# Moving ScalarE's low-half gate copies from behind their one-hots into the next two weight chunks

## The chip, the cores and the metric

The kernel runs on one core of a Trainium2 chip. The core has five engines that run beside each other, each through its own instructions in the order in which they were written down: TensorE (PE, matmuls into PSUM), VectorE (DVE), ScalarE (ACT), GpSimd (POOL, here the indirect row gathers) and SyncE (SP, here nearly all other transfers). An engine that comes to an instruction whose input is not there waits, and all behind it on that engine waits too. The metric is the time of one execution in microseconds (us); lower is better.

## The reference, cut to what matters

One layer of a streaming encoder block over 512 tokens of width 1024: a mixer with two head groups, then a channel sub-layer that picks single-neuron experts, then a norm. The change touches the expert part alone:

```
q = (xb @ w_q).reshape(p, PEER_HEADS, 2, PEER_DK_HALF)
sc = jnp.einsum('phcd,hcnd->phcn', q, sub_keys).astype(jnp.float32)
top_s, top_i = lax.top_k(sc, PEER_TOPK)
cand_s = (top_s[:, :, 0, :, None] + top_s[:, :, 1, None, :]).reshape(p, PEER_HEADS, kk)
cand_i = (top_i[:, :, 0, :, None] * N_KEYS + top_i[:, :, 1, None, :]).reshape(p, PEER_HEADS, kk)
best_s, best_pos = lax.top_k(cand_s, PEER_TOPK)
idx = jnp.take_along_axis(cand_i, best_pos, axis=-1)
g = jax.nn.softmax(best_s, axis=-1)
u_sel = expert_u[idx]
act = jax.nn.gelu(jnp.einsum('phkd,pd->phk', u_sel, xb), approximate=False)
coef = (g * act.astype(jnp.float32)).astype(xb.dtype)
return jnp.einsum('phk,phkd->pd', coef, expert_v[idx])
```

Each token has 8 heads with 16 experts each, 128 of the 16384 = 128 x 128 experts. An expert is named by a pair of numbers, one from each half of the keys.

## The kernel before

**Dense and sparse tokens.** 192 of the 512 tokens are handled sparsely: their experts' rows are fetched by indirect DMA (L753) and VectorE takes dot products with them (L774). The other 320 tokens are handled densely: all 16384 activations are computed as matmuls with the whole of `expert_u`, and the picked ones are kept by multiplying with a gate matrix that is zero elsewhere.

**The u chunks.** `expert_u` comes in 128 chunks of 512 KB. The matmuls work with a split: ScalarE copies a chunk to a rounded high half (`whi`, `w_high`, L78), VectorE subtracts to get the low half (`wlo`, `w_low`, L83), and TensorE does three products per block, 24 matmuls in all (L92 to L94), into one of two accumulators (`ps_act`, `bufs=2`). ScalarE empties the accumulator with a gelu (`u_evict`, L841); this is written down one chunk later, so chunk k's matmuls need the eviction of chunk k - 2, which stands in ScalarE's list in chunk k - 1.

**The gates.** For 8 tokens at a time a gate step (`gates_step`) prepares and multiplies. The preparation (`gates_prep`) has VectorE make one-hots of both key numbers (L626) and multiply one of them with the high part of the gate (L631); ScalarE makes the same product with the low part of the gate, in eight copies with a scale (L633 and L634, the "low copies"). They go to the second half of the tile `igh`. The gate matmuls (`gates_mm`, L645) use high and low product, and they are written down one gate step later than the preparation. The gate evictions to a staging tile (`gates_out`, L654) and the store of a full tile (`gates_store`, L665) follow one step after that. There are 40 such steps of 8 tokens, and at the end 16 of 4 tokens in another form without low copies.

**The order of the work** is written out by hand (`manual_schedule`). The loop over the first `CE` = 124 chunks writes down, for chunk k: the load of chunk k + 5 on SyncE and the low half of chunk k + 2 on VectorE (`weights`), chunk k's matmuls and the eviction of chunk k - 1 (`u_chunk`), then VectorE work from four generators (searches, rest of the searches, gates, dots) until the planner's counter of VectorE time has caught up with TensorE's, and last the high half of chunk k + 3 (`w_high`). The planner chooses by counters (`pe`, `dve`, `ac`) and due times, all fixed when the program is built. Most gate steps fall into every second chunk, some into neighbouring ones. In ScalarE's list one chunk with a gate step thus reads: eviction of chunk k - 1, eight low copies, two gate evictions of the step before, high half of chunk k + 3.

After these chunks come the rest of u and the 128 chunks of `expert_v` (L1020), not touched by the change.

Of the kernel before, what the change touches and what calls it, by code (L numbers as in the profile page):

```python
# [2 lines left out]

# [10 lines left out]
AF = mybir.ActivationFunctionType  # L14
# [20 lines left out]
def block_kernel(ctx, tc, xT, small, w_ada1, w_ada, b_ada, w_in, w_r, w_i, w_out, w_q, keys, uT, u, v, final_g, out):  # L35
    nc = tc.nc
# [53 lines left out]
    def mm3(ps, hi, lo, xh, xl, ks, first, last):  # L90
        for k in ks:
            nc.tensor.matmul(ps, hi[:, k, :], xh(k), start=first and k == ks[0], stop=False)  # L92
            nc.tensor.matmul(ps, hi[:, k, :], xl(k), start=False, stop=False)  # L93
            nc.tensor.matmul(ps, lo[:, k, :], xh(k), start=False, stop=last and k == ks[-1])  # L94
# [226 lines left out]
    for cb in range(4):  # L321
# [16 lines left out]
        ig = mt("ig")  # L338
# [274 lines left out]
    def gates_prep(sl, t0, wide):  # L613
        oh = topk.tile([128, 8, 128], F32, name="oh8", bufs=2)
        if not wide:
            nc.vector.tensor_tensor(oh[:, 0:4, :], iota[:, None, :].to_broadcast([128, 4, 128]),
                                    sl[:, 1, t0:t0 + 4, None].to_broadcast([128, 4, 128]), op=OP.is_equal)
            for k in range(4):
                nc.vector.tensor_scalar(oh[:, 4 + k, :], iota, sl[:, 0, t0 + k:t0 + k + 1], sl[:, 2, t0 + k:t0 + k + 1],
                                        op0=OP.is_equal, op1=OP.mult)  # L620
            return oh, None
        sij, gh, gl = sl
        flat = oh.rearrange("p a b -> p (a b)").bitcast(F16)
        a0 = slice(t0 // 2, t0 // 2 + 4)
        shp = [128, 8, 128, 2]
        nc.vector.tensor_tensor(flat.rearrange("p (q n b) -> p q n b", q=8, b=2), io2[:, None, :, :].to_broadcast(shp),  # L626
                                sij[:, a0].rearrange("p a w b -> p (a w) b")[:, :, None, :].to_broadcast(shp),
                                op=OP.is_equal)
        of = flat.rearrange("p (a w n b) -> p a w n b", a=4, w=2, b=2)
        ig = topk.tile([128, 2, 4, 128, 2], F16, name="igh", bufs=2)  # L630
        nc.vector.tensor_tensor(ig[:, 0], of[:, :, 0], gh[:, a0][:, :, None, :].to_broadcast([128, 4, 128, 2]), op=OP.mult)  # L631
        for k in range(8):
            nc.scalar.activation(ig[:, 1, k // 2, :, k % 2], of[:, k // 2, 0, :, k % 2], AF.Copy,  # L633
                                 scale=gl[:, t0 + k:t0 + k + 1])  # L634
        return of, ig

    def gates_mm(oh, ig, k0):
        pg = psE.tile([128, 4, 128], F32, name="ps_gt", bufs=4)
        for k in range(4):
            a, b = divmod(k0 + k, 2)  # L640
            if ig is None:
                nc.tensor.matmul(pg[:, k, :], oh[:, k, :], oh[:, 4 + k, :], start=True, stop=True)
            else:
                for w in range(2):
                    nc.tensor.matmul(pg[:, k, :], oh[:, a, 1, :, b], ig[:, w, a, :, b], start=w == 0, stop=w == 1)  # L645
        return pg
# [3 lines left out]
    def gates_out(t, t0, pg, scale):  # L650
        gq, q4 = divmod(t0 // 4, 4)
        if q4 == 0:
            gst[t] = stgp[0].tile([128, 128, 16], F32, name="stg", bufs=2)
        nc.scalar.activation(gst[t][:, :, q4 * 4:q4 * 4 + 4], pg.rearrange("p t n -> p n t"), AF.Copy, scale=scale)  # L654
        if q4 == 3:
            stores.append((t, gq, gst[t]))
# [3 lines left out]
    def gates_store():  # L660
        while stores:
            t, gq, st = stores.pop()
            for e in (1, 0):
                eng = nc.scalar if (t, gq) == (1, 3) else nc.sync
                eng.dma_start(Gd[t][gq][:, 64 * e:64 * e + 64, :], st[:, 64 * e:64 * e + 64, :])  # L665

    def gates_step(item):
        if item is not None:
            t, sl, t0, wide = item
            gpre.append((t, t0, gates_prep(sl, t0, wide)))  # L670
        gates_store()
        for _ in range(len(gpost)):
            gates_out(*gpost.pop(0))
        if len(gpre) > (item is not None):
            t, t0, (oh, ig) = gpre.pop(0)
            for k0 in range(0, 4 if ig is None else 8, 4):
                gpost.append((t, t0 + k0, gates_mm(oh, ig, k0), 1.0 if ig is None else 1.0 / GS))
                pe[0] += 890 if ig is None else GPE

    def gates_tile(t, groups, sl, wide=True):  # L680
        step = 8 if wide else 4
        for t0 in range(groups[0] * 16, groups[-1] * 16 + 16, step):
            gates_step((t, sl, t0, wide))
            ac[0] += 510 * step if wide else 120 * step
            given["g"] += step // 4
            yield 1780 if wide else 1680
# [63 lines left out]
    def gath(table, idxs, k, key):  # L750
        if key not in rows:
            r = row_tile()
            nc.gpsimd.indirect_dma_start(out=r[:, :], out_offset=None, in_=table,  # L753
                                         in_offset=bass.IndirectOffsetOnAxis(ap=idxs[:, k:k + 1], axis=0))
            rows[key] = r
# [59 lines left out]
    def w_high(k):  # L815
        if k < len(jobs):
            whi[k] = high(wraw[k])
# [5 lines left out]
    def weights(k):  # L823
        w_load(k + 5)
        w_low(k + 2)
# [4 lines left out]
    def spill(q):  # L830
        nc.sync.dma_start(Ad[q], act[q].rearrange("p c t -> p (c t)"))
        act[q] = None
# [3 lines left out]
    def u_evict():  # L836
        if unread:
            c, ps = unread.pop()
            if c % 2 == 0:
                act[c // 2] = ring.tile([128, 2, NU], F32, name="act", bufs=RB // 2)  # L840
            nc.scalar.activation(act[c // 2][:, c % 2], ps, AF.Gelu)  # L841

    def u_chunk(k, pool):
        c = jobs[k][1]
        ps = pool.tile([128, NU], F32, name="ps_act", bufs=2)
        mm3(ps, whi.pop(k), wlo.pop(k), hd, ld, range(KB), True, True)
        u_evict()
        unread.append((c, ps))
        q = c // 2 - RB // 2 + 2
        if c % 2 == 0 and 0 <= q < v0 // 2:  # L850
            spill(q)
        pe[0] += 3530
        dve[0] += 1140
        ac[0] += 1400
# [99 lines left out]
    for k in range(CE):  # L954
        weights(k)
        u_chunk(k, psE)
        cur[0] = k
        if sready and not first:
            first.append(k + 4)
            asleep["d"] = k + 4  # L960
            for m in range(GB_E - 1):
                gath(u, usteps[m][0], usteps[m][3], m)
        ac[0] = max(ac[0], pe[0] - LEAD)
        dve[0] = max(dve[0], RHO * pe[0] - LEAD - (HEAD if k < 9 else 0))
        xd = 0
        while dve[0] < RHO * pe[0] or k == KD:
            g = turn(k)
            if k == KD:
                g = next((g for g in "sg" if g in gens), None)
                if "s" not in gens and len(bdone) < XB:  # L970
                    g = "d"
            if g is None or (g == "d" and "g" not in gens and xd >= XD):
                break
            n = next(gens[g], 0)
            if n == 0:
                assert g != "d"
                late_k[g] = k
                del gens[g]
                continue
            if n is None:  # L980
                asleep[g] = k + 1
                continue
            dve[0] += n
            xd += g == "d"
            if gopen or g == "d":
                given[g] += {"g": 0, "d": 1}.get(g, n)
        w_high(k + 3)
        if k == KD:
            ep.close()
            vp = ctx.enter_context(tc.tile_pool(name="vp", bufs=2, reuse_waits="tile"))  # L990
            gp = ctx.enter_context(tc.tile_pool(name="gp", bufs=1, reuse_waits="tile"))
            late[:] = [gp, taken[0] + 10]
            gt8 = vp.tile([128, 2, NG, 8, 16], F32, name="gt", bufs=1)
        m = k - CE + XE
        if 0 <= m < XE:
            for n in [0] if m < 2 else range(5) if m == XE - 1 else [8]:
                v_gates(n)
        if m >= XE - 2:
            (v_gated, v_rest)[m - XE + 2](0)
# [37 lines left out]
    for k in range(CE, len(jobs)):  # L1037
# [3 lines left out]
        kind, n = jobs[k]  # L1041
# [25 lines left out]
    g2r, _, fgr = frow  # L1067
# [107 lines left out]
```

## Time and profile before

| what | us |
|---|---|
| median of 3 runs (lowest, highest) | 1497.47 (1497.16, 1499.59) |
| the profiled execution: time, span | 1498.0, 1496.2 |
| TensorE matmul busy | 1352.5 (90%) |
| VectorE busy | 1225.6 (82%) |
| ScalarE busy | 686.6 (46%) |
| GpSimd busy | 507.3 (34%) |
| high halves L78, ScalarE | 308.4 |
| low halves L83, VectorE | 356.0 |
| dots L774, VectorE (192 of them) | 234.5 |
| one-hots L626, VectorE | 48.8 |

Busy times overlap, since the engines run beside each other. A row of a costly group reads: line, engine, operation, output and inputs with shapes, count, then busy time and the mean in ns of one, then the idle time of that engine just before these instructions and what ended most of it. A row of the list of waits reads: engine and line that waited, engine and line that it waited for, total us, times, longest. In a timeline row stand start and length in us, and in brackets the idle time before it. In a row of windows the columns are named in its first line; "PEclk" is the clock granted to TensorE as a share of full speed, "DMA share" the busy share of the core's 16 DMA engines.

### The profile page before, as it was taken

Reading aid. Unit: us, or ns where it says so; the run is one execution under the profiler, and the core shown is the slowest. Engines: PE = TensorE matmul, PEld = TensorE weight load, DVE = VectorE, ACT = ScalarE, POOL = GpSimd, SP = SyncE. Lnnn points to the kernel's source line nnn. Section 1 sums busy time; section 2 is a strip of 40 time slices with the busy share of each in tenths; the row PEclk is TensorE's granted clock in tenths of the full one; section 3 lists DMA queues with packets and bytes.
Section 4 is the critical chain, followed back from the end, with each engine's and each line's share of the span. In section 5 each row is a group of like instructions: output and inputs, shape, how many; then the busy total and the mean of one; then the engine's idle time right before and its main releaser. Section 6 shows DMA issues by size and latency. Waiting matters only on the chain.

```text
span 1496.2 us, 21797 instructions
## 1 busy us (share of the span) xinstructions
PE 1352.5 (90%) x7739; PEld 1158.2 (77%) x7739; DVE 1225.6 (82%) x2332; ACT 686.6 (46%) x1178; POOL 507.3 (34%) x334
## 2 busy tenths in 40 slices
PE   5999999989888877878788997999999999999996
PEld 2666786889888877878777996787788888888885
DVE  6765655999787767878777997698998899999998
ACT  4544434444456566566555442334334343333333
POOL 0000000001132023231445355465666575555540
PEclk9999999999999898999999998999999999999998
DMA  9666222235577778888999999999999999999994
GB/s 375 215 234 211 95 89 71 85 113 168 184 232 267 243 241 289 284 268 280 312 360 326 355 388 381 339 381 378 415 410 414 408 416 413 414 414 402 391 338 164
DMA packets 146929, 440.07 MB, mean 294 GB/s; under 512 B 14722, under 2 KB 42370, under 8 KB 144772
## 3 DMA queue, kind: packets, MB, share of 16 engines
q1 hardware_dynamic: 99812, 267.75, 49.8%
q0 software_dynamic: 46720, 169.89, 29.8%
q8 instruction: 60, 0.98, 0.3%
q10 hardware_dynamic: 288, 1.05, 0.2%
q14 instruction: 49, 0.40, 0.1%
HBM read 393.54 MB, written 45.09 MB: 293 GB/s over the span
## 4 chain that ended last, share of the span: by engine, by line
PE 41%; issue 26%; DVE 13%; DMA 12%; POOL 7%; ACT 1%; DVEq 0%; POOLq 0%; SPq 0%; ACTq 0%
PE acc L1020 26%; POOL rows L753 7%; DMA rows<-in_u_dram,idx_s 6%; DMA wraw<-in_v_dram 4%; PE ps_z L92 4%; PE ps_z L94 4%; PE ps_z L93 4%; DVE wlo L83 2%; DVE scr L774 2%; DMA rows<-in_u_dram,idx_b 1%; PE ps_row L136 1%; DVE rep L457 1%; DVE ti L455 1%; DVE ti L462 1%; DVE top L460 1%
## 5 line engine op out<-in xcount | busy, mean ns | idle before, releaser
L78 ACT ACTIVATE whi<-wraw 128x1024 fp32r<-128x1024 f32 x292 | 308.4, 1057 | 427.1 <-PE acc L1020 174.0
L83 DVE TENSOR_TENSOR wlo<-wraw,whi 128x1024 fp32r<-128x1024 f32 x292 | 356.0, 1221 | 174.2 <-ACT whi L78 173.0
L92 PE MATMUL ps_act<-h,whi 128*128 128x320 f32 x1024 | 334.7, 327 | 83.3 <-ACT act L841 82.1
L94 PE MATMUL ps_act<-h,wlo 128*128 128x320 f32 x1024 | 325.0, 317 | 2.9 <-DVE wlo L83 2.9
L93 PE MATMUL ps_act<-h,whi 128*128 128x320 f32 x1024 | 324.9, 317 | 0.0
L92 PEld LDWEIGHTS ps_act<-h,whi 128*128 128x128 f32 x1024 | 200.6, 196 | 93.0 <-ACT act L841 91.4
L753 POOL DMA_INDIRECT rows<-in_u_dram,idx_s x128 | 201.5, 1574 | 168.0 <-DVE scr L774 145.2
L753 POOL DMA_INDIRECT rows<-in_v_dram,idx_s x128 | 203.6, 1591 | 155.3 <-DVE ys L790 136.2
L1020 PE MATMUL acc<-whi,ch 128*128 128x512 f32 x750 | 232.6, 391 | 11.4 <-ACT act L841 10.7
L1020 PE MATMUL acc<-whi,cl 128*128 128x512 f32 x750 | 232.2, 391 | 3.0 <-DVE cl L917 2.8
L1020 PE MATMUL acc<-wlo,ch 128*128 128x512 f32 x750 | 232.1, 391 | 0.4 <-DVE wlo L83 0.4
L753 POOL DMA_INDIRECT rows<-in_u_dram,idx_b x64 | 97.0, 1515 | 344.6 <-DVE scr L774 260.6
L94 PEld LDWEIGHTS ps_act<-h,wlo 128*128 128x128 f32 x1024 | 200.0, 195 | 3.5 <-DVE wlo L83 3.4
L93 PEld LDWEIGHTS ps_act<-h,whi 128*128 128x128 f32 x1024 | 201.0, 196 | 0.2
L633 ACT ACTIVATE igh<-oh,gl 128x128 f16<-128x128 f16 x320 | 99.7, 428 | 162.2 <-DVE oh L626 162.2
L1020 PEld LDWEIGHTS acc<-whi,ch 128*128 128x128 f32 x750 | 140.9, 188 | 41.9 <-ACT act L841 11.5
L774 DVE SCALAR_TENSOR_TENSOR scr<-rows,h2n 128x1024 f16<-128x1024 f32 x128 | 156.4, 1222 | 18.0 <-DMA rows<-in_u_dram,idx_s 16.6
L1020 PEld LDWEIGHTS acc<-whi,cl 128*128 128x128 f32 x750 | 140.8, 188 | 34.6 <-DVE cl L917 5.5
L1020 PEld LDWEIGHTS acc<-wlo,ch 128*128 128x128 f32 x750 | 141.3, 188 | 30.3 <-DVE wlo L83 0.8
L790 DVE SCALAR_TENSOR_TENSOR ys<-rows,acts,ys 128x1024 f32<-128x1024 f32 x127 | 162.7, 1281 | 1.4
L408 POOL DMA_DIRECT2D x1d<-xn x8 | 4.5, 568 | 281.1 <-DVE wlo L83 234.4
L92 PE MATMUL ps_z<-h,whi 128*128 128x512 f32 x224 | 90.8, 409 | 2.7 <-ACT h L216 2.4
(261 smaller groups left out, 1684.6 us busy)
## 6 DMA issues: line engine op xcount, KB each, us to landing
wraw<-in_uT_dram SPq DMA_DIRECT2D x128, 512.0 KB, 6.0
wraw<-in_v_dram SPq DMA_DIRECT2D x128, 512.0 KB, 9.3
Gd<-stg SPq DMA_DIRECT2D x46, 512.0 KB, 7.4
wada<-in_w_ada_dram SPq DMA_DIRECT2D x16, 1024.0 KB, 5.3
Ad<-act SPq DMA_DIRECT2D x48, 320.0 KB, 6.6
act<-Ad SPq DMA_DIRECT2D x48, 320.0 KB, 11.4
h<-Gd SPq DMA_DIRECT2D x12, 1024.0 KB, 15.7
wraw<-in_w_in_dram SPq DMA_DIRECT2D x20, 512.0 KB, 6.3
```

Source lines behind the costliest of these rows:

```text
L78: nc.scalar.activation(hi, raw, AF.Copy)
L83: nc.vector.tensor_sub(lo, raw, hi.bitcast(F32))
L92: nc.tensor.matmul(ps, hi[:, k, :], xh(k), start=first and k == ks[0], stop=False)
L93: nc.tensor.matmul(ps, hi[:, k, :], xl(k), start=False, stop=False)
L94: nc.tensor.matmul(ps, lo[:, k, :], xh(k), start=False, stop=last and k == ks[-1])
L136: nc.tensor.matmul(pr[32 * b:32 * b + 1, :], cs[:, k:k + 1], wt[:, b * 512:(b + 1) * 512], start=(k == 0), stop=(k == KB - 1), skip_group_ ...
L455: nc.vector.max_index(out=where[:, 0:8], in_max=best[:, 0:8], in_values=s)
L633: nc.scalar.activation(ig[:, 1, k // 2, :, k % 2], of[:, k // 2, 0, :, k % 2], AF.Copy, scale=gl[:, t0 + k:t0 + k + 1])
L753: nc.gpsimd.indirect_dma_start(out=r[:, :], out_offset=None, in_=table, in_offset=bass.IndirectOffsetOnAxis(ap=idxs[:, k:k + 1], axis=0))
L774: nc.vector.scalar_tensor_tensor(scr, rows.pop(n), 1.0, hn, op0=OP.mult, op1=OP.mult, accum_out=dst[:, k:k + 1])
L790: nc.vector.scalar_tensor_tensor(ys, rows.pop(k), acts[:, k:k + 1], ys, op0=OP.mult, op1=OP.add)
L1020: nc.tensor.matmul(accs[b][e], st[:, bs], mv[:, e * 512:(e + 1) * 512], start=first, stop=last)
```

## The change

`gates_prep` no longer writes down the eight low copies; it puts the tiles that they need on a list. A new function `gates_low(n)` writes down up to n copies from that list, oldest first. It is called with 4 in each u chunk, right behind that chunk's `u_chunk`, and with 8 ahead of each gate step, so that a step's copies stand before the gate matmuls that read them and before the next preparation. The counters of the planner are not changed.

```diff
-from itertools import chain
+from itertools import chain, cycle
...
-        for k in range(8):
-            nc.scalar.activation(ig[:, 1, k // 2, :, k % 2], of[:, k // 2, 0, :, k % 2], AF.Copy,
-                                 scale=gl[:, t0 + k:t0 + k + 1])
+        lows.append((of, ig, gl, t0))
         return of, ig
+
+    lows = []
+
+    def gates_low(n):
+        for _ in range(n):
+            if lows:
+                of, ig, gl, t0 = lows[0]
+                k = next(low_k)
+                nc.scalar.activation(ig[:, 1, k // 2, :, k % 2], of[:, k // 2, 0, :, k % 2], AF.Copy,
+                                     scale=gl[:, t0 + k:t0 + k + 1])
+                if k == 7:
+                    lows.pop(0)
+
+    low_k = cycle(range(8))
...
         for t0 in range(groups[0] * 16, groups[-1] * 16 + 16, step):
+            gates_low(8)
             gates_step((t, sl, t0, wide))
...
         u_chunk(k, psE)
+        gates_low(4)
         cur[0] = k
```

## The prediction

> **What bounds the kernel now.** I read the page's costliest groups first, then the list of waits cut into the stretch where the changed line runs, then one period of that stretch in the timeline, engine by engine.
>
> ```profile
> L83 DVE TENSOR_TENSOR wlo<-wraw,whi 128x1024 fp32r<-128x1024 f32 x292 | 356.0, 1221 | 174.2 <-ACT whi L78 173.0
> L92 PE MATMUL ps_act<-h,whi 128*128 128x320 f32 x1024 | 334.7, 327 | 83.3 <-ACT act L841 82.1
> L633 ACT ACTIVATE igh<-oh,gl 128x128 f16<-128x128 f16 x320 | 99.7, 428 | 162.2 <-DVE oh L626 162.2
> L1020 PE MATMUL acc<-whi,ch 128*128 128x512 f32 x750 | 232.6, 391 | 11.4 <-ACT act L841 10.7
> ```
>
> Three waits form a ring. ScalarE stands 162.2 us in front of the low copies (L633) until VectorE has the one-hot; TensorE stands 82.1 us in front of a new u chunk until ScalarE has emptied an accumulator (L841); VectorE stands 173.0 us until ScalarE has made a high half (L78). The 320 low copies are 40 gate steps of eight. The answer for their line gives durations (min/median/max) and the first and last start:
>
> ```profile
> L633 ACT ACTIVATE igh<-oh,gl x320: 418/426/448, 387.3 to 806.6; 128x128 f16<-128x128 f16 x160
> ```
>
> Only between 387 and 807 us does the change act. The list of waits over three stretches of it:
>
> ```profile
> PE ps_act L92 <- ACT act L841: 39.2, 13, 7.0
> DVE wlo L83 <- ACT whi L78: 50.9, 19, 6.0
> PE ps_act L92 <- ACT act L841: 16.9, 9, 3.1
> DVE wlo L83 <- ACT whi L78: 16.1, 8, 3.1
> PE ps_act L92 <- ACT act L841: 23.1, 11, 3.6
> DVE wlo L83 <- ACT whi L78: 22.8, 11, 2.9
> ```
>
> The pairs of rows are 387 to 600, 600 to 700 and 700 to 820 us (total, times, longest). TensorE's 39.2, 16.9 and 23.1 add to 79.2, nearly all of the 82.1: here lies what can be won. Busy times of the same stretches, and of two later ones:
>
> ```profile
> core 0: us, PE busy (x) PEld busy (x) DVE busy (x) ACT busy (x) POOL busy (x), PEclk, DMA share, GB/s
> 387.00:600.00 213.00, 171.22 (x1228) 166.16 (x1229) 160.06 (x334) 131.62 (x289) 51.83 (x35) 0.90 0.74 245
> 600.00:700.00 100.00, 83.15 (x625) 79.74 (x624) 78.45 (x169) 61.50 (x137) 31.34 (x20) 0.97 0.84 284
> 700.00:820.00 120.00, 96.90 (x726) 92.98 (x725) 92.46 (x125) 68.92 (x160) 53.93 (x35) 0.99 0.92 326
> 820.00:900.00 80.00, 76.32 (x551) 76.08 (x550) 73.52 (x146) 34.37 (x53) 35.69 (x25) 0.98 0.99 372
> 1200.00:1300.00 100.00, 100.00 (x443) 82.81 (x442) 94.44 (x88) 40.79 (x52) 62.67 (x37) 1.00 1.03 414
> ```
>
> Neither TensorE nor VectorE is full between 387 and 820 us, each at about 75 to 83%: they wait for each other in turn, through ScalarE. One period, two u chunks with one gate step, ScalarE first, then VectorE, then TensorE:
>
> ```profile
> 724.18 1.05 ACT L78 ACTIVATE whi<-wraw 128x1024 fp32r<-128x1024 f32 x1
> 725.13 0.43 ACT L841 ACTIVATE act<-ps_act 128x320 f32<-128x320 f32 x1
> 730.00 2.49 ACT L633 ACTIVATE igh<-oh,gl 128x128 f16<-128x128 f16 x8 [4.45 <-DVE oh L626]
> 732.36 1.05 ACT L654 ACTIVATE stg<-ps_gt 128x512 f32<-128x512 f32 x2
> 733.31 1.05 ACT L78 ACTIVATE whi<-wraw 128x1024 fp32r<-128x1024 f32 x1
> 734.26 0.42 ACT L841 ACTIVATE act<-ps_act 128x320 f32<-128x320 f32 x1
> ```
>
> ```profile
> 724.00 1.23 DVE L83 TENSOR_TENSOR wlo<-wraw,whi 128x1024 fp32r<-128x1024 f32 x1 [2.62 <-ACT whi L78]
> 725.14 1.22 DVE L774 SCALAR_TENSOR_TENSOR scr<-rows,h2b 128x1024 f16<-128x1024 f32 x1
> 728.69 1.22 DVE L626 TENSOR_TENSOR oh<-io,selT 128x2048 f16<-128x2048 f16 x1
> 734.39 1.23 DVE L83 TENSOR_TENSOR wlo<-wraw,whi 128x1024 fp32r<-128x1024 f32 x1 [2.62 <-ACT whi L78]
> 736.80 1.22 DVE L774 SCALAR_TENSOR_TENSOR scr<-rows,h2b 128x1024 f16<-128x1024 f32 x1
> ```
>
> ```profile
> 724.34 0.42 PE L92 MATMUL ps_act<-h,whi 128*128 128x320 f32 x1 [2.11 <-ACT act L841]
> 727.96 1.09 PE L645 MATMUL ps_gt<-igh,oh 128*128 128x128 f16 x16
> 734.73 0.41 PE L92 MATMUL ps_act<-h,whi 128*128 128x320 f32 x1 [2.11 <-ACT act L841]
> ```
>
> The chain can be followed by its start times: one-hot at 728.69, ready at 729.91; eight low copies from 730.00; two gate evictions at 732.36; high half at 733.31; accumulator emptied from 734.26 to 734.68; TensorE goes on at 734.73. The eviction needed only matmuls that had ended long before; its place in ScalarE's order kept it back. The period is 10.39 us, of which TensorE worked 10.39 - 2.11 = 8.28 and VectorE 10.39 - 2.62 = 7.77.
>
> **The change, part by part.** *The copies themselves*: the same 320, none added. Four and four instead of eight in a run is 2 x 1.24 us instead of 2.49: nothing.
>
> *Removed: ScalarE's stop.* A step's copies now stand behind the evictions of the next two chunks. With a step every second chunk, ScalarE has in the step's chunk an eviction (0.42), four copies of the step before (1.24), two gate evictions (1.05) and a high half (1.05), 3.76 us, and in the other chunk 0.43 + 1.24 + 1.05 = 2.72. Together 6.48, under TensorE's 8.28. In the step's chunk no entry waits any longer for that chunk's VectorE work. A chunk's matmuls take 727.96 - 724.34 = 3.62 us, so its accumulator is empty about 3.76 + 0.42 = 4.2 us after they began, and TensorE wants it again at 8.28: TensorE's wait should go altogether. High halves come earlier too, since they no longer follow a one-hot.
>
> *Added: a new place for the wait.* The gate matmuls of a step come after the chunk two further on, 3.62 us into it; ScalarE ends the second four copies 0.42 + 1.24 = 1.66 us into it. Cover 1.96 us, cost nothing; if the cover is gone, TensorE waits there for the difference. Where two steps come in neighbouring chunks, all eight stand in one chunk and end at 0.42 + 2.48 = 2.90 us, still ahead. Where two steps share one chunk, the flush puts the copies behind the one-hot as now:
>
> ```profile
> 490.08 2.48 ACT L633 ACTIVATE igh<-oh,gl 128x128 f16<-128x128 f16 x8 [4.56 <-DVE oh L626]
> 492.44 1.05 ACT L654 ACTIVATE stg<-ps_gt 128x512 f32<-128x512 f32 x2
> 493.39 2.48 ACT L633 ACTIVATE igh<-oh,gl 128x128 f16<-128x128 f16 x8
> ```
>
> That is the only pair I find so close. On VectorE, GpSimd and the load queue no instruction changes its place; the planner's counters are fed as before. The stores on SyncE follow the gate evictions, which come earlier. Nothing queued behind the moved copies is urgent beyond what is counted above.
>
> *Recovered: the clock.* After a long stop TensorE is slow for some 5 us:
>
> ```profile
> 391.10 0.64 PE L92 MATMUL ps_act<-h,whi 128*128 128x320 f32 x1 [5.43 <-ACT act L841]
> 391.53 0.47 PE L93 MATMUL ps_act<-h,whi 128*128 128x320 f32 x1
> 396.33 0.31 PE L94 MATMUL ps_act<-h,wlo 128*128 128x320 f32 x1
> 396.48 0.30 PE L92 MATMUL ps_act<-h,whi 128*128 128x320 f32 x1
> ```
>
> Starts are 0.27 us apart at first and 0.15 later. The first stretch was granted 0.90, so its 171.2 us of TensorE work would take about 154 at full clock; the second 83.15 x 0.97 = 81, the third 96.9 x 0.99 = 96.
>
> *What is late next.* First stretch: TensorE 154, VectorE 160, so VectorE. It will still wait for some high halves: of the chain from one-hot to high half (1.22 + 2.49 + 1.05 + 1.05 = 5.8 us) gate evictions and the high half itself, 2.1, stay. I keep three tenths of its 50.9, 15 us: 160 + 15 = 175. Bounds 160 and 213. Gain 38.
>
> Second stretch: TensorE 81, VectorE 78.5 + 0.3 x 16.1 = 83.3. Take 84; bounds 81 and 100. Gain 16.
>
> Third stretch: TensorE 96, VectorE 92.5 + 0.3 x 22.8 = 99.3, but the transfers come near their end. The stretch moved 326 GB/s x 120 us = 39.1 MB. At 372, which 820 to 900 us shows with the same kinds of loads, stores and row gathers, this takes 105; at the 414 of a stretch that hardly stores, 94.5; by the share, 120 x 0.92 / 0.99 = 111.5. The row gathers say the same from another side:
>
> ```profile
> rows<-in_u_dram,idx_s POOLq DMA_INDIRECT x30, 7.7
> rows<-in_u_dram,idx_s POOLq DMA_INDIRECT x25, 9.3
> ```
>
> These are the gathers of 700 to 820 and of 820 to 900 us, with their median time to landing. There are four row buffers: the one that the dot at 725.14 frees at 726.36 feeds the dot at 736.80, 10.4 us later. In a period of 8.3 us this becomes about 8.3: enough for 7.7, short by 1.0 for 9.3. A period of 9.3 makes the stretch 120 x 9.3 / 10.4 = 107. I take 107; bounds 96 and 120. Gain 13.
>
> The Trainium skill (DMA: Bandwidth & Descriptors, "Where 436 GB/s comes from") says that traffic between HBM and SBUF is bound at about 358 GB/s for a core; by that the third stretch would take an estimated 326 x 120 / 358 = 109 us, and the sum below would be 65 instead of 67. The row from 1200 to 1300 us, 414 GB/s on one core, does not agree with it as a ceiling; by 414 the transfers would cover nothing, VectorE's 99 would bind, and the sum would be 75.
>
> *Behind 820 us* nothing is moved. TensorE's waits there, 10.7 us in the page's L1020 row, come from transfers; I leave them, between all gone and doubled.
>
> *The sum*: 38 + 16 + 13 = 67 us. The profiled execution took 1498.0 us (span 1496.2), so 1431; the median of the runs is 0.5 us lower: 1430.5.
>
> **Rivals.** *TensorE or VectorE bare, no residue*: 213 - 160 = 53, 100 - 81 = 19, 120 - 96 = 24, together 96, 1402. For it: ScalarE has room and every long TensorE wait is on L841. Against it: the transfer share of 0.92 in the third stretch, and work per chunk that is uneven in the first.
>
> *The transfers and the four row buffers take over early*: VectorE then waits for rows where it waited for high halves. If the third stretch gains nothing, the second half of its 16, and the first 27 (half of its bound), that is 35: 1463. For it: the share stands at 0.84 and 0.92 already, and faster periods bring more gathers at once. Against it: in 820 to 900 us TensorE was 76.3 of 80 us busy at a share of 0.99.
>
> *The change does not do what it says*: the flush ahead of each step finds all copies still unissued, and they wait as now; 1498. It needs steps that share a chunk; I see one such pair among 40 steps.
>
> *Slower: the wait moves to the gate matmuls.* If ScalarE runs behind TensorE by L at the chunk in question, TensorE waits L - 1.96 us for the second four copies at each step. It decides from where 40 x (L - 1.96) exceeds the 96 us that the ring costs now, L = 4.4 us. At a lag of a whole chunk with its gate matmuls, 3.62 + 1.09 = 4.71, it costs 110: 1498 - 96 + 110 = 1512. Against it: ScalarE has 6.48 us of work in 8.28 and nothing left that stops it so long.
>
> **How the numbers follow.** Forecast 0.57, own range 1417 to 1447; bare engines 0.17; transfers early 0.20; no effect 0.03; slower 0.03. From 1404 to 1463 about two cases in ten are left out, most of them just past either end. A difference of 0.2%, 3 us, is what a measurement of this kernel can tell from none. Faster 0.94, same 0.03, slower 0.03.
>
> **What would show it.** Right: the idle time of L633 for the one-hot falls from 162 to under 40 us and that of L92 for L841 from 82 to under 15; the clock between 387 and 600 us rises to 0.97 or more; the last low copy starts some 65 us earlier than 806.6; the transfer share in the last third reaches about 1 and VectorE's waits for rows there grow. Wrong: a wait of gate matmuls (L645) for the low copies, L841 still in front of L92, or the won time given back by transfers behind 740 us.

## The result and the profile after

The changed kernel takes 1417.05 us (median of 4 runs, 1416.97 to 1418.94) against 1497.51 for the kernel before: a ratio of 0.9463 with a 95% interval of 0.9447 to 0.9479, 80 us faster. The forecast was 1430.5 us, 67 us faster, with a range of 1404 to 1463.

The costliest groups of the changed kernel; the low copies are now line 642 and the eviction of a u accumulator line 854:

```profile
L83 DVE TENSOR_TENSOR wlo<-wraw,whi 128x1024 fp32r<-128x1024 f32 x292 | 355.8, 1220 | 88.4 <-ACT whi L78 87.4
L92 PE MATMUL ps_act<-h,whi 128*128 128x320 f32 x1024 | 326.4, 319 | 10.1 <-ACT act L854 6.4
L1034 PE MATMUL acc<-whi,ch 128*128 128x512 f32 x750 | 232.6, 391 | 9.0 <-ACT act L854 8.7
L642 ACT ACTIVATE igh<-oh,gl 128x128 f16<-128x128 f16 x320 | 104.7, 430 | 71.0 <-DVE oh L626 71.0
```

TensorE's wait for the eviction fell from 82.1 to 6.4 us, VectorE's for the high half from 173.0 to 87.4. What is left of the latter lies outside the gate steps. ScalarE still stands 71.0 us in front of its low copies, but hardly anybody waits for that any more (the gate matmuls, 5.9 us in all).

The same three pieces of work as in the prediction, now from 387 to 550, 550 to 632 and 632 to 737 us:

```profile
387.00:550.00 163.00, 158.50 (x1235) 154.85 (x1234) 157.43 (x334) 129.09 (x284) 57.49 (x35) 0.99 0.88 318
550.00:632.00 82.00, 77.17 (x591) 75.52 (x590) 77.53 (x168) 62.70 (x141) 31.16 (x19) 0.96 0.94 338
632.00:737.00 105.00, 100.70 (x753) 96.16 (x752) 91.91 (x125) 69.99 (x161) 52.43 (x36) 0.98 0.98 378
```

They took 213, 100 and 120 us before and take 163, 82 and 105 now: 50, 18 and 15 won, 83 in all, of which 3 are given back right behind. The bounds between them do not fall on the same instruction before and after: the second window holds 591 of TensorE's instructions instead of 625, the third 753 instead of 726. The table of the next section is cut at the same work. In the first, TensorE (158.5) and VectorE (157.4) are both busy for 97% of the time; in the third the transfer engines are, with a share of 0.98.

One period of the third stretch, ScalarE and then VectorE; in brackets stands the idle time ahead:

```profile
648.14 0.44 ACT L854 ACTIVATE act<-ps_act 128x320 f32<-128x320 f32 x1
651.00 1.32 ACT L642 ACTIVATE igh<-oh,gl 128x128 f16<-128x128 f16 x4 [2.41 <-DVE oh L626]
652.19 1.04 ACT L78 ACTIVATE whi<-wraw 128x1024 fp32r<-128x1024 f32 x1
653.14 0.41 ACT L854 ACTIVATE act<-ps_act 128x320 f32<-128x320 f32 x1
653.45 1.30 ACT L642 ACTIVATE igh<-oh,gl 128x128 f16<-128x128 f16 x4
654.63 1.05 ACT L666 ACTIVATE stg<-ps_gt 128x512 f32<-128x512 f32 x2
655.58 1.05 ACT L78 ACTIVATE whi<-wraw 128x1024 fp32r<-128x1024 f32 x1
656.53 0.41 ACT L854 ACTIVATE act<-ps_act 128x320 f32<-128x320 f32 x1
```

```profile
649.68 1.22 DVE L626 TENSOR_TENSOR oh<-io,selT 128x2048 f16<-128x2048 f16 x1
652.69 1.22 DVE L83 TENSOR_TENSOR wlo<-wraw,whi 128x1024 fp32r<-128x1024 f32 x1
655.23 1.23 DVE L787 SCALAR_TENSOR_TENSOR scr<-rows,h2b 128x1024 f16<-128x1024 f32 x1 [0.17 <-DMA rows<-in_u_dram,idx_b]
656.38 1.22 DVE L83 TENSOR_TENSOR wlo<-wraw,whi 128x1024 fp32r<-128x1024 f32 x1
657.52 1.22 DVE L626 TENSOR_TENSOR oh<-io,selT 128x2048 f16<-128x2048 f16 x1
```

From one-hot to one-hot it is 7.84 us here instead of 10.4. The low half at 652.69 starts before the high half at 652.19 is even finished: it uses one made a chunk earlier. ScalarE waits 2.41 us for the one-hot, and no row of VectorE here has a wait for ScalarE. The only bracket in VectorE's rows is 0.17 us for a row gather.

### The profile page after: what moved, and what is told of

Same layout as the page of the kernel before. It is cut to its first block, busy times and chain, and to the rows that moved or that the text cites. A ratio compares the mean times of both kernels' runs of the same rounds, so it can differ in the third digit from the quotient of the medians.

```text
span 1417.2 us, 21765 instructions
## 1 busy us (share of the span) xinstructions
PE 1340.4 (95%) x7739; PEld 1149.2 (81%) x7739; DVE 1221.6 (86%) x2332; ACT 688.0 (49%) x1178; POOL 516.6 (36%) x334
## 4 chain that ended last, share of the span: by engine, by line
PE 30%; DVE 21%; DMA 16%; issue 11%; POOL 2%; ACT 2%; DVEq 0%; SPq 0%; POOLq 0%; ACTq 0%
PE acc L1034 27%; DMA rows<-in_u_dram,idx_s 7%; DVE wlo L83 5%; DVE scr L787 3%; DMA wraw<-in_v_dram 3%; DMA rows<-in_u_dram,idx_b 2%; DMA wraw<-in_uT_dram 2%; POOL rows L766 2%; DVE oh L626 1%; DVE rep L457 1%; DVE ti L455 1%; DVE ti L462 1%; DMA act<-Ad 1%; DVE top L460 1%; ACT whi L78 1%
## 5 line engine op out<-in xcount | busy, mean ns | idle before, releaser
L83 DVE TENSOR_TENSOR wlo<-wraw,whi 128x1024 fp32r<-128x1024 f32 x292 | 355.8, 1220 | 88.4 <-ACT whi L78 87.4
L92 PE MATMUL ps_act<-h,whi 128*128 128x320 f32 x1024 | 326.4, 319 | 10.1 <-ACT act L854 6.4
L94 PE MATMUL ps_act<-h,wlo 128*128 128x320 f32 x1024 | 321.6, 314 | 5.3 <-DVE wlo L83 5.3
L93 PE MATMUL ps_act<-h,whi 128*128 128x320 f32 x1024 | 320.5, 313 | 0.0
L766 POOL DMA_INDIRECT rows<-in_v_dram,idx_s x128 | 207.8, 1624 | 152.3 <-DVE ys L803 127.4
L766 POOL DMA_INDIRECT rows<-in_u_dram,idx_s x128 | 198.0, 1547 | 162.3 <-DVE scr L787 143.2
L92 PEld LDWEIGHTS ps_act<-h,whi 128*128 128x128 f32 x1024 | 196.6, 192 | 13.2 <-ACT act L854 7.7
L94 PEld LDWEIGHTS ps_act<-h,wlo 128*128 128x128 f32 x1024 | 196.2, 192 | 7.4 <-DVE wlo L83 7.4
L766 POOL DMA_INDIRECT rows<-in_u_dram,idx_b x64 | 105.5, 1649 | 263.5 <-DVE scr L787 179.4
L93 PEld LDWEIGHTS ps_act<-h,whi 128*128 128x128 f32 x1024 | 196.5, 192 | 0.1
L642 ACT ACTIVATE igh<-oh,gl 128x128 f16<-128x128 f16 x320 | 104.7, 430 | 71.0 <-DVE oh L626 71.0
```

Source lines behind the costliest of these rows:

```text
L83: nc.vector.tensor_sub(lo, raw, hi.bitcast(F32))
```

## The experiments

All kernels below differ from the one before or the changed one by a few lines. "Chunk c to chunk d" is the time between the starts of ScalarE's evictions of these u chunks, the same work in each kernel; these four columns come from one profiled execution of each:

| kernel | us | ratio to before (95%) | 17 to 57 | 57 to 76 | 76 to 98 | 98 to 104 |
|---|---|---|---|---|---|---|
| before | 1497.5 | | 220.3 | 104.4 | 109.7 | 32.2 |
| changed | 1417.05 | 0.9463 (0.9447 to 0.9479) | 169.7 | 83.6 | 96.1 | 36.0 |
| b_acc3 | 1499.65 | 1.0004 (0.9991 to 1.0017) | 220.4 | 105.1 | 107.5 | 33.5 |
| b_high | 1431.67 | 0.9552 (0.9530 to 0.9574) | 182.1 | 88.6 | 94.3 | 32.5 |
| b_both | 1431.99 | 0.9560 (0.9536 to 0.9585) | 183.5 | 88.7 | 92.3 | 35.1 |
| b_const | 1418.33 | 0.9460 (0.9436 to 0.9484) | 168.5 | 82.6 | 99.1 | 36.9 |
| a_end | 1422.35 | 0.9490 (0.9469 to 0.9512) | 176.0 | 86.1 | 94.3 | 35.0 |
| a_eight | 1417.22 | 0.9471 (0.9445 to 0.9496) | 172.2 | 82.4 | 94.8 | 36.4 |
| a_high | 1414.03 | 0.9442 (0.9419 to 0.9465) | 169.8 | 82.8 | 97.1 | 35.6 |
| a_best | 1416.35 | 0.9450 (0.9430 to 0.9470) | 170.5 | 82.0 | 96.5 | 33.9 |
| a_half | 1407.84 | 0.9406 (0.9383 to 0.9430) | 168.0 | 82.5 | 92.0 | 33.2 |
| a_load | 1416.64 | 0.9458 (0.9434 to 0.9482) | 170.6 | 84.4 | 101.4 | 29.6 |

**Two links or one?** The prediction spoke of a ring of three engines. Looking at the start times again there are two candidates for what closes it: the eviction (TensorE waits) and the high half (VectorE waits). b_acc3 gives TensorE a third accumulator in the kernel before:

```diff
-        ps = pool.tile([128, NU], F32, name="ps_act", bufs=2)
+        ps = pool.tile([128, NU], F32, name="ps_act", bufs=3 if pool is psE else 2)
```

> The kernel before with a third u accumulator (ps_act, three buffers instead of two in the first 124 chunks); the low copies stay behind their one-hots. Theory A: what sets the period is a loop of VectorE and ScalarE alone: one-hot, low copies, gate evictions, high half, low half, two dots, low half, next one-hot; TensorE's wait for the eviction is only a consequence of it. Then a third accumulator changes nothing that lasts: 1490 to 1499 us, and VectorE's wait for the high half stays near 90 us in the gate stretch. Theory B: the late eviction of the accumulator is what holds the ring: TensorE gets a chunk of room, its wait for L841 goes, and the time falls to 1420 to 1445.

Nothing changed: 1499.65, ratio 1.0004 (theory A's range ended at 1499). The list of waits from 387 to 820 us of b_acc3:

```profile
ACT igh L633 <- DVE oh L626: 165.6, 39, 8.4
DVE wlo L83 <- ACT whi L78: 88.4, 37, 6.0
PE ps_act L92 <- ACT act L841: 31.7, 27, 5.5
PEld ps_act L94 <- DVE wlo L83: 24.2, 37, 1.3
PE ps_gt L645 <- ACT stg L654: 22.8, 24, 4.3
```

And of the kernel before over the same time:

```profile
DVE wlo L83 <- ACT whi L78: 89.9, 38, 6.0
PE ps_act L92 <- ACT act L841: 79.1, 33, 7.0
```

TensorE's wait for the eviction fell from 79.1 to 31.7 us, and the rest came up elsewhere: in front of the low halves and of the gate evictions. VectorE's 89.9 and 88.4 did not move. A period in b_acc3, VectorE and then ScalarE:

```profile
719.72 1.22 DVE L626 TENSOR_TENSOR oh<-io,selT 128x2048 f16<-128x2048 f16 x1
725.43 1.22 DVE L83 TENSOR_TENSOR wlo<-wraw,whi 128x1024 fp32r<-128x1024 f32 x1 [2.62 <-ACT whi L78]
726.57 1.22 DVE L774 SCALAR_TENSOR_TENSOR scr<-rows,h2b 128x1024 f16<-128x1024 f32 x1
727.83 1.22 DVE L774 SCALAR_TENSOR_TENSOR scr<-rows,h2b 128x1024 f16<-128x1024 f32 x1
728.98 1.22 DVE L83 TENSOR_TENSOR wlo<-wraw,whi 128x1024 fp32r<-128x1024 f32 x1
```

```profile
721.03 2.49 ACT L633 ACTIVATE igh<-oh,gl 128x128 f16<-128x128 f16 x8 [4.45 <-DVE oh L626]
723.39 1.05 ACT L654 ACTIVATE stg<-ps_gt 128x512 f32<-128x512 f32 x2
724.35 1.05 ACT L78 ACTIVATE whi<-wraw 128x1024 fp32r<-128x1024 f32 x1
```

The wait is 2.62 us to the hundredth as before. The loop closes without TensorE: one-hot, low copies, gate evictions, high half, low half, two dots, low half, next one-hot, each starting as the one ahead of it ends.

The other way round, b_high cuts that link alone, in the kernel before:

```diff
         u_chunk(k, psE)
+        w_high(k + 3)
         cur[0] = k
...
                 given[g] += {"g": 0, "d": 1}.get(g, n)
-        w_high(k + 3)
```

> The kernel before with the high half of chunk k + 3 written down right behind the chunk's matmuls and eviction, ahead of the gate work, instead of at the chunk's end; the low copies stay behind their one-hots. Theory A (loop of VectorE and ScalarE through the high half): the loop is cut, VectorE runs on, one-hots come early, and 1415 to 1440 us follow although the eviction still stands behind the low copies. Theory B (the eviction behind the low copies holds the ring): it still stands there, so not below 1475.

1431.67, 67 of the 80 us, with the eviction still behind the low copies. So the high half was the link that held. TensorE's wait for the eviction is 28.7 us here:

```profile
PE ps_act L92 <- ACT act L841: 28.7, 14, 5.1
```

**Work or wait?** b_const keeps ScalarE's copies where they were and takes away only what they wait for. It leaves the low part of the gates out of the result:

```diff
-            nc.scalar.activation(ig[:, 1, k // 2, :, k % 2], of[:, k // 2, 0, :, k % 2], AF.Copy,
+            nc.scalar.activation(ig[:, 1, k // 2, :, k % 2], io2[:, :, k % 2], AF.Copy,
```

> The kernel before with the eight low copies in their old place, but reading a constant tile instead of the one-hots: it leaves the low part of the gates out of the result, ScalarE's work and order stay. If the wait for the one-hot is what costs (theories A and B alike): 1410 to 1435 us. If the 2.5 us of copying in that place cost by themselves, ahead of the high half and the eviction: not below 1470.

1418.33, the changed kernel's time within its interval. The 2.5 us of copying cost nothing in their old place; the wait in front of them cost it all.

**The last 14 us of b_high.** Because of those 28.7 us, b_both adds the third accumulator to it (both diffs above together).

> The kernel before with both edits, the high half ahead of the gate work and a third u accumulator; the low copies stay behind their one-hots. b_high ended 14 us above the changed kernel and still shows 28.7 us of TensorE waiting for the eviction. If those 14 us are the eviction's place behind the low copies, a third accumulator takes them away: 1414 to 1422 us. If something else holds them (the one-hot wait itself, gate evictions behind it): 1427 to 1433.

1431.99: the first guess fell. The wait for the eviction went down to 7.4 us and the time did not move:

```profile
PE ps_act L92 <- ACT act L841: 7.4, 4, 4.5
```

A search chunk of b_high shows what was left; first ScalarE, then VectorE:

```profile
437.34 2.49 ACT L633 ACTIVATE igh<-oh,gl 128x128 f16<-128x128 f16 x8 [2.28 <-DVE oh L626]
439.70 1.05 ACT L654 ACTIVATE stg<-ps_gt 128x512 f32<-128x512 f32 x2
440.66 1.90 ACT L568 ACTIVATE oh<-pf 128x2048 f16<-128x2048 f16 x1
442.57 1.28 ACT L571 ACT_TABLE_LOAD   x1
```

```profile
442.59 1.23 DVE L573 TENSOR_TENSOR oh<-oh,st 128x2048 f16<-128x2048 f16 x1 [2.33 <-ACT oh L568]
446.90 1.22 DVE L83 TENSOR_TENSOR wlo<-wraw,whi 128x1024 fp32r<-128x1024 f32 x1 [1.83 <-ACT whi L78]
```

The searches' wide copy (L568) is something else that VectorE waits for (5.1 us in three places in b_high), and it still stood behind the low copies. a_end puts the low copies of the changed kernel last in their own chunk, behind everything:

```diff
         u_chunk(k, psE)
-        gates_low(4)
...
         w_high(k + 3)
+        gates_low(8)
```

> The changed kernel with the low copies in their step's own chunk again, but as ScalarE's last entry of it, behind the searches' copies and exponentials, the gate evictions and the high half; the next chunk's eviction of the accumulator stands behind them, as in the kernel before. Theory A, as b_both leaves it: what counts is that nothing that VectorE waits for stands behind the low copies (high half, and in the search chunks the wide copy L568); the 14 us by which b_high stayed above the changed kernel are that search work: 1412 to 1422 us. Rival: the copies have to leave their chunk, because they wait for that chunk's one-hot in front of the next eviction: 1428 to 1440.

1422.35, just past the end of what theory A allowed. So 9 of the 14 us came from the low copies standing ahead of other ScalarE work of the same chunk; that VectorE and the gate matmuls wanted that work is read from waits like those above. The other 5 are hardly clear of the noise, since the intervals of a_end and the changed kernel touch. If they are real, they may lie in the place of the next eviction. From 387 to 554 and from 554 to 740 us of a_end:

```profile
PE ps_act L92 <- ACT act L854: 9.9, 6, 4.5
DVE wlo L83 <- ACT whi L78: 3.1, 4, 1.5
PE ps_act L92 <- ACT act L854: 12.0, 12, 2.5
```

TensorE waits 21.9 us for evictions again, against 6.4 in all of the changed kernel. But b_both has shown that such a wait can go and win nothing, and a third accumulator in a_end was not tried, so the place of the 5 us is not shown.

**Four and four, or eight?** a_eight calls `gates_low(8)` behind `u_chunk` instead of `gates_low(4)`.

> The changed kernel with all eight low copies in the next chunk instead of four in each of the next two. Theory A: only being off the step's own chunk counts, the spreading nothing: 1413 to 1423 us. Rival: the spreading counts, since a run of 2.5 us stands ahead of the high half and the eviction in one chunk: 1425 to 1445.

1417.22, no difference. The spreading is not what helps.

**Is there more?** a_high is b_high's edit on the changed kernel; a_best adds the third accumulator to it.

> The changed kernel with the high half ahead of low copies and gate work as well. Theory A: after the change the high half is in time already (1.8 us of waiting for it left between 387 and 550 us), so nothing more is to be had: 1413 to 1420 us. Rival, the residue that the prediction kept in the first stretch is real and lies in the high half: 1402 to 1410.

> The changed kernel with the high half ahead of the low copies and with a third u accumulator, an attempt to beat it. Theory A: VectorE and TensorE are both at 97% of the time between 387 and 550 us already and the transfers bind later, so at most 4 us: 1411 to 1418. Rival, ScalarE's order still costs in the search chunks: 1400 to 1410.

1414.03 and 1416.35; both intervals overlap that of the changed kernel, so neither is shown to beat it.

**What binds the third stretch?** The prediction let the transfers take 11 of the 24 us that were open there. a_half makes the first 92 gathers half as long; a_load adds traffic. The main lines of the two edits:

```diff
-            nc.gpsimd.indirect_dma_start(out=r[:, :], out_offset=None, in_=table,
+            half_row = table is u and key < NHALF
+            nc.gpsimd.indirect_dma_start(out=r[:, :512] if half_row else r[:, :], out_offset=None,
+                                         in_=table.rearrange("n (a d) -> (n a) d", a=2) if half_row else table,
...
+        if 20 <= k < 42 or 76 <= k < 98:
+            nc.sync.dma_start(xtra[k], uT[k][:, 0:2, :].rearrange("p k e -> p (k e)"))
```

> The changed kernel with the first 92 row gathers of half the bytes (512 of 1024 elements of a row, from other places; the dots read the half twice, so VectorE's work stays; the sparse results are not the reference's). If the transfers or the landing of rows bind the third stretch (u chunks 76 to 98, 96.1 us in the changed kernel), it falls to 90 to 93 and the first stretch (chunks 17 to 57, 169.7 us) moves by less than 3; time 1406 to 1413. If VectorE and TensorE bind it, both stretches stay within 1 us: 1415 to 1419.

> The changed kernel with an extra copy of 128 KB from HBM to HBM in each of u chunks 20 to 41 and 76 to 97, which nobody reads. If the transfers bind the third stretch and not the first: chunks 76 to 98 grow by 5 to 10 us, chunks 17 to 57 by less than 2.5; time 1422 to 1430. If they bind neither: both grow by less than 2, 1416 to 1420.

Chunks 76 to 98 fell from 96.1 to 92.0 us with shorter gathers and rose to 101.4 with the extra copies; chunks 17 to 57 moved by 1.7 and 0.9. The windows of that stretch, of a_half and of a_load:

```profile
629.00:721.00 92.00, 90.60 (x708) 87.79 (x707) 85.59 (x117) 64.95 (x153) 51.47 (x32) 1.00 0.89 310
```

```profile
634.00:736.00 102.00, 94.82 (x704) 91.73 (x702) 90.38 (x124) 66.19 (x155) 52.99 (x35) 0.97 1.02 396
```

With 310 GB/s moved, TensorE is busy for 90.6 of 92 us; with 396 the share stands at 1.02 and TensorE waits. So the transfers do bind there, for about 4 us of the 96. That size is rough: the fast kernels with the full gathers and no added traffic lie between 92.3 and 99.1 us in this column. The waits say by what way. Over these chunks VectorE waits 9.7 us for gathered rows in the changed kernel and 5.5 in a_half; in a_load ScalarE waits 21.7 us for u chunks to load, against 1.9. The whole of a_half, 1407.84, is 9 us faster, clear of the noise.

In a_load the time of the whole was missed, though: 1416.64 instead of 1422 to 1430. What chunks 76 to 98 lost, chunks 98 to 104 gave back (36.0 to 29.6 us). In that place ScalarE waits for a staging tile to be stored, in the changed kernel and in a_load:

```profile
ACT stg L666 <- DMA Gd<-stg: 10.9, 1, 10.9
PE ps_gt L654 <- DVE oh L619: 5.5, 1, 5.5
```

```profile
ACT stg L666 <- DMA Gd<-stg: 8.7, 1, 8.7
PE ps_gt L654 <- DVE oh L619: 3.5, 1, 3.5
```

The stop of the changed kernel ends at 751.30 and that of a_load at 752.84, 1.5 us later, although chunk 98 came 6.0 us later there: 4.5 of the 6.4 us are made up by the end of the stop; the rest stays open. The same eviction has a stop in the kernel before as well:

```profile
832.24 1.09 ACT L654 ACTIVATE stg<-ps_gt 128x512 f32<-128x512 f32 x2 [9.02 <-PE ps_gt L642]
751.30 0.60 ACT L666 ACTIVATE stg<-ps_gt 128x512 f32<-128x512 f32 x1 [10.85 <-DMA Gd<-stg]
```

The first row, of the kernel before, names matmuls, but those that this eviction reads had started at 824.96 and taken 1.17 us. What came late was the store there too: the trace has its last landing at 831.85, 11.7 us after its issue at 820.12. In the changed kernel it is issued at 739.63 and has landed at 751.20, 11.6 us later. So the store is no slower; it is issued 10.4 us after the eviction of chunk 98 began instead of 7.0, and these 3.4 us are most of the 3.8 given back. A third staging tile was not tried.

## Why the prediction was right, and where its steps were not

**The number**: 1417.05 is 13 us below the forecast, at the very rim of the prediction's own range of 1417 to 1447. The sum used no wait of TensorE: it was built from each engine's work as a bound, a part of VectorE's wait for the high half, and the transfers. So the wrong ring did not get into it.

**Where the time is won**: right. All of it lies between the first and the last low copy: by the table 85.0 us between the evictions of chunks 17 and 98 (83 by the windows, whose bounds are not cut at the same instruction), of which 3.8 go back by chunk 104; 80 are left at the end.

**First stretch, 38 forecast, 50 measured.** The term that failed is "I keep three tenths of its 50.9, 15 us". VectorE's wait for the high half there is

```profile
DVE wlo L83 <- ACT whi L78: 1.8, 1, 1.8
```

from 387 to 550 us. A wait that belongs to a closed loop is not shared out among the loop's members when one is taken away. Once the loop is open, the high half is there a chunk ahead, and the wait is gone unless a longer chain takes its place. The bound of 160 us, VectorE's own work, was nearly reached: 163.

**Second and third stretch**: 84 forecast and 82 measured, 107 and 105; cut at the same work, by the table, the gains are 20.8 and 13.6 us where 16 and 13 were forecast. In part this is luck. The same residue, 4.8 and 6.8 us of waiting for the high half, did not come here either: from 550 to 737 us no such wait of VectorE is left. In the second stretch TensorE's own 81 us stood close to the forecast. In the third the transfers were let to take 11 us above TensorE's 96, and a_half gave some 4 back. The time of that stretch agrees with what the 372 GB/s of 820 to 900 us said, 105; the window shows 378. The ceiling of about 358 GB/s that the Trainium skill gives for traffic between HBM and SBUF (DMA: Bandwidth & Descriptors, "Where 436 GB/s comes from") did not hold on this one core, with 378 in the changed kernel. The 396 of a_load contain its copies from HBM to HBM.

**The ring of three**: wrong as a mechanism. The 79.2 us of TensorE's waits were called what can be won; b_acc3 took 47 of them away and won nothing. They were a shadow of the loop between VectorE and ScalarE. That they are nearly as large as the gain (83) fits TensorE and VectorE having nearly the same amount of work, 158.5 and 157.4 us in the first stretch; no run tests it.

**The new place of the wait**: forecast at nothing. The gate matmuls wait for the low copies 5.9 us in five places:

```profile
PE ps_gt L657 <- ACT igh L642: 5.9, 5, 3.5
```

**The clock**: right in size. From 387 to 550 us it was granted at 0.99 instead of 0.90. Before, seven stops of TensorE of 3.0 to 7.0 us in the first stretch were followed by a few us with starts 0.27 us apart; now one is, and it is only 1.95 us long:

```profile
438.24 0.42 PE L92 MATMUL ps_act<-h,whi 128*128 128x320 f32 x1 [1.95 <-ACT act L854]
```

So "after a long stop" is not the whole of it: the stops of 2.11 us in the prediction's period are followed by starts 0.15 us apart. What decides is open.

**"L633's idle time under 40"**: wrong, 71.0. ScalarE still reaches the copies before VectorE has made the one-hot. It costs little: a_high cut it to 33.1 us, and its time is 3 us lower, within the noise.

**Behind 820 us**: forecast unchanged; 3.8 us lost by chunk 104, most of it because a staging tile is stored later. The prediction put TensorE's 10.7 us of waits there down to transfers, but its row names the eviction; it is 8.7 us now.

## What to carry to other kernels

To find what holds a period, follow start times from one instruction to its next copy until the chain closes, and see which engines are in it. An engine with a large wait outside that chain gains nothing from more buffers. On an engine that works in order, an instruction that waits for a neighbour should stand behind everything that this neighbour waits for; that alone was worth 75 of the 80 us here (a_end), while the 2.5 us of copying (b_const) and how they were cut (a_eight) did not matter.

## What the runs showed of the hardware beyond the forecast

With TensorE, VectorE and the transfers all near their ends, 378 GB/s (the changed kernel) and 396 (a_load) of loads, stores and gathers mixed were carried for some 100 us on end, at a share of 0.98 and 1.02, while TensorE was busy for 96 and 93% of the time. Just behind that stretch the store of a staging tile, two transfers of 512 KB, took 11.6 us to land, and 11.7 in the kernel before; ScalarE stood 10.85 and 9.02 us there.
